# Raw weight quarters of a second attention unit in the exponentials' tiles, and of the first output half in a row tile

## The chip, the cores and the metric

The kernel runs on one core of a Trainium2 chip. It is one launch that computes a whole decoder layer. The metric is device time in microseconds (us): the median of three runs before is 1226.28 us (1226.03 to 1226.78). One further execution was profiled; all rows below come from it.

## The reference

The layer has a sequence of 1024 rows and 1024 columns, all in float32. Cut to what matters here:

```python
h = rms_norm(x, norm1_w[l])
proj = h @ w_in[l]
da_q, da_k, da_v, dn_qkv, dn_z, dn_a, dn_b = jnp.split(proj, [...], axis=-1)
da_q = rms_norm(da_q.reshape(B, S, DA_HEADS, 2, DA_QK_DIM), q_norm_w[l])
da_k = rms_norm(da_k.reshape(B, S, DA_HEADS, 2, DA_QK_DIM), k_norm_w[l])
da_o = diff_attention(da_q, da_k, da_v, lam)          # two softmax maps per head, 4 heads
...
dn_o = gated_delta_rule(dn_q, dn_k, dn_v, g, beta)    # chunked scan, 4 heads
...
mix = jnp.concatenate([da_o.reshape(B, S, DA_WIDTH), dn_o.reshape(B, S, DN_WIDTH)], axis=-1)
x = x + mix @ w_out[l]
h = rms_norm(x, norm2_w[l])
x = x + jnp.square(jax.nn.relu(h @ w_up[l])) @ w_down[l]
```

## The kernel before

Every large product is made of three TensorE products: an operand is split into a rounded part (H) and the rest (L), and HH, HL and LH are added up in PSUM. A weight is therefore loaded raw by DMA, ScalarE casts it to the rounded part (`wH`, L213) and VectorE or GpSimd subtracts to get the rest (`wL`, L214). `load_unit` (L199) does that in quarters: DMA into a raw buffer, cast, subtraction.

The stages follow each other: the first projections; the DeltaNet heads' projections; then, between 213 and 444 us, a stage in which several streams share TensorE; then the output projection, still beside attention; then the MLP from about 615 us to the end.

In the shared stage run: `horner` (a triangular inverse, in four tiles of the tag `pexp`), `scan` and `scan_out` (the DeltaNet scan in eight chunks), `da_units` (attention's projections), `da_turns` (their transposes, L947 and L948, and the split of what comes out into `qa`, L954 and L955), `scores` (L1130 to L1149) and `values` (L1171 to L1190). The order of TensorE's instructions is written out by a planner, the class `Interleave`: streams with priorities run against a modelled clock, and `unit_time` (L753) tells it when each quarter of a weight is due. The other engines' orders are set by the framework's scheduler from dependences; each engine, and SP's queue of DMA issues, then works its own list in order.

`da_units` works on three weight units of 512 columns. A unit has two halves of the contraction, `kh` 0 and 1, each of four k steps; a k step is three matmuls of 512 columns (L994, L995, L996). Eight token tiles go through in four pairs, so a unit is 64 k steps; below, "second unit, step 5" counts them from 0 in the order in which they are made: two tiles' `kh` 0 (four steps each), then their `kh` 1. Each finished tile is copied out of one of two PSUM banks by ScalarE (`qn`, L1022). A half's weights for the next unit may be cast as soon as the last pair is through with that half, and they are due when the next unit's first pair comes to them.

A raw quarter before has one of two buffers:

```python
raw = rp.tile([P, 2 * UC], F32, tag="wraw", name="wraw", bufs=5) if rp else laid("wraw")
```

`laid("wraw")` has two buffers, so the third and the fourth quarter of a half can only be fetched once the first and the second have been subtracted. The planner has the same in `start = flow.now if i < 2 else done[i - 2]`.

A turn (L947, L948) needs one of two PSUM banks of the tag `px`, which is free again when VectorE has made the last `qa` rest (L955) of the turn two before it.

After the scan, a pool of eight row tiles holds the accumulators of the eight token tiles (`accs`), into which x is loaded ahead (L935) and to which the output projection's halves are added (L1280).

Of the kernel before, what the change touches and what calls it, by code (L numbers as in the profile page):

```python
# [9 lines left out]
F32 = mybir.dt.float32  # L10
# [8 lines left out]
P = 128  # L19
SEQ = 1024  # L20
DM = 1024
KB = DM // P
NT = SEQ // P
# [5 lines left out]
UC = 260  # L29
# [103 lines left out]
def tile_hymba_layer(  # L133
# [7 lines left out]
    V, S, G, T = nc.vector, nc.scalar, nc.gpsimd, nc.tensor  # L141
# [3 lines left out]
    w_in_v = w_in[0].rearrange("(kb p) c -> p kb c", p=P)  # L145
    w_out_v = w_out[0].rearrange("(kb p) c -> p kb c", p=P)
# [17 lines left out]
    def laid(tag):  # L164
        if tag in ahead:
            return ahead.pop(tag)
        pool, shape, dt, bufs = FORMS[tag]
        return pool.tile(shape, dt, tag=tag, name=tag, bufs=bufs)
# [27 lines left out]
    hH = hpool.tile([P, KB, SEQ], F32R, name="hH")  # L196
    hL = hpool.tile([P, KB, SEQ], F32R, name="hL")

    def load_unit(src, ranges, k0=0, nk=KB, eng=None, rp=None):  # L199
        eng = eng or G  # L200
        width = sum(n for _, n in ranges)
        wh, wl = staged("wH"), staged("wL")
        wh = wh[:, :nk * width].rearrange("p (k c) -> p k c", k=nk)
        wl = wl[:, :nk * width].rearrange("p (k c) -> p k c", k=nk)
        st = 2 * UC // width
        for k in range(0, nk, st):
            raw = rp.tile([P, 2 * UC], F32, tag="wraw", name="wraw", bufs=5) if rp else laid("wraw")
            raw = raw[:, :st * width].rearrange("p (k c) -> p k c", k=st)
            o = 0
            for c0, n in ranges:  # L210
                nc.sync.dma_start(raw[:, :, o:o + n], src[:, k0 + k:k0 + k + st, c0:c0 + n])
                o += n
            S.copy(wh[:, k:k + st, :], raw)  # L213
            eng.tensor_tensor(wl[:, k:k + st, :], raw, wh[:, k:k + st, :].bitcast(F32), ALU.subtract)  # L214
        return wh, wl
# [144 lines left out]
    with tc.manual_schedule(engines={T.engine, V.engine, S.engine}):  # L360
# [37 lines left out]
        raw = n1.tile([P, NT, UC], F32, name="zr")  # L398
# [17 lines left out]
    for tb in range(NT):  # L416
        T.matmul(tail[:, 300 + 2 * tb:302 + 2 * tb], ssum_[:, tb * P:(tb + 1) * P], ones[:, 0:2],
                 start=True, stop=True)
# [310 lines left out]
    ae = actx.enter_context(tc.tile_pool(name="ae", bufs=4, **right))  # L729
# [16 lines left out]
    flow = Interleave()  # L746
# [3 lines left out]
    HF = (slice(0, 64), slice(64, 128))  # L750
    MM, TR = 219.0, 110.0

    def unit_time(eng="G", rate=1230.0):  # L753
        done = []
        for i in range(4):
            start = flow.now if i < 2 else done[i - 2]
            done.append(flow.chain(("S", 520.0), (eng, rate), start=start + DMA_T))
        return done

# [112 lines left out]
    def scan_out(c, Sold, yy):  # L872
        pkb = {}
        for h in range(HEADS):
            pkb[h] = sb.tile([P, 2, P], F32, tag="pkb", name="pkb", bufs=5)
            nc.sync.dma_start(pkb[h], park_d[h, c, :, 3:5, :])
        zgt = sb.tile([P, 512], F32, tag="zgt", name="zgt", bufs=1)
        nc.sync.dma_start(zgt, zg_d[c])
        flow.begun(("oc", c % 2))
        oc = sb.tile([P, 512], F32, tag="oc", name="oc", bufs=2)  # L880
        so = sb.tile([P, 4], F32, tag="so", name="so", bufs=2)
        osq = sb.tile([P, P], F32, tag="osq", name="osq", bufs=1)
        yield flow.now + 2500, "pB"
        if c > 0:
            o1 = pB.tile([P, 512], F32, tag="pB", name="ps_o1")
            for h in range(HEADS):
                T.matmul(o1[:, h * P:(h + 1) * P], pkb[h][:, 0, :], Sold[h], start=True, stop=True)
            V.tensor_tensor(v4(oc), v4(o1), bc_col(eg[:, c::8]), ALU.mult)
            flow.pe(4 * MM)
            flow.hold("pB", flow.chain(vec(512)))  # L890
            yield flow.now, "pB"
        o2 = pB.tile([P, 512], F32, tag="pB", name="ps_o2")
        for h in range(HEADS):
            T.matmul(o2[:, h * P:(h + 1) * P], pkb[h][:, 1, :], yy[h], start=True, stop=True)
        if c > 0:
            V.tensor_tensor(oc, oc, o2, ALU.add)
        else:
            S.copy(oc, o2)
        for h in range(HEADS):
            i = cidx(h, c)  # L900
            S.activation(osq, oc[:, h * P:(h + 1) * P], AF.Square, scale=rq[:, i:i + 1], accum_out=so[:, h:h + 1])
        f = sb.tile([P, 4], F32, tag="of", name="of", bufs=2)
        rstd(f, so, 1.0 / P, EPS, sb, "oft", 4)
        V.tensor_tensor(f, f, rqr[:, c::8], ALU.mult)
        for h in range(HEADS):
            V.scalar_tensor_tensor(oc[:, h * P:(h + 1) * P], oc[:, h * P:(h + 1) * P], f[:, h:h + 1],
                                   zgt[:, h * P:(h + 1) * P], ALU.mult, ALU.mult)
        flow.pe(4 * MM)
        t = flow.chain(vec(512))
        flow.hold("pB", t)  # L910
        t = flow.chain(*[act(P, True)] * 4, vec(4), powr(4), vec(4), *[vec(P, 60)] * 4, start=t)
        flow.put_off(t, ("oc", c % 2), lambda: nc.sync.dma_start(mixn_d[c], oc))
        if c == NT - 1:
            yield t + DMA_T, None
            flow.begun(("oc", c % 2))
            s2ctx.close()
            spctx.close()
            mp = ctx.enter_context(tc.tile_pool(name="mp", bufs=1, **left))
            pools["mp"] = mp
            for tb in tiles:  # L920
                accs[tb] = row_tile("acc")
            pools["a2"] = bctx.enter_context(tc.tile_pool(name="a2", bufs=1, **left))
            pools["be"] = bctx.enter_context(tc.tile_pool(name="be", bufs=2, **left))
            pools["rsc"] = scctx.enter_context(tc.tile_pool(name="rsc", bufs=1, space=PSUM, **right))
            state["scan"] = True

    def row_tile(name):
        return pools["mp"].tile([P, DM], F32, tag="row", name=name, bufs=8)

    def prefetch_x(after):  # L930
        if state["scan"] and state["xs"] < NT:
            tb = state["xs"]
            state["xs"] += 1
            with tc.issue_after(after.ins):
                nc.sync.dma_start(accs[tb], x2[tb * P:(tb + 1) * P, :])  # L935
# [33 lines left out]
    def da_units():  # L969
        todo = [[(512, 256), (0, 256)], [(1024, 256), (768, 256)], [(1280, 256), (256, 256)]]  # L970

        def half_w(src, ranges, k0):
            return load_unit(src, ranges, k0, 4, eng=V), unit_time("V", 610.0)

        w = [(w, [0.0] * 4) for w in first_w]
        freed = [0.0, 0.0]
        for i in range(3):
            if i == 1:
                vts[0] = ap.tile([P, NT, P], F32, tag="vt", name="vt")
            for pair in range(NT // 2):  # L980
                pss = {}
                for kh in range(2):
# [18 lines left out]
                            freed[j] = yield from leave(i, tb, ps)  # L1001
                    if pair == NT // 2 - 1:
                        if i < 2:
                            w[kh] = half_w(w_in_v, todo[i + 1], 4 * kh)
                        elif kh == 0:
                            pre.append(half_w(w_out_v, [(0, 512)], 4))
        pctx.close()
        state["proj"] = True

# [251 lines left out]
    def outproj():  # L1261
# [39 lines left out]

        w0 = pre[0]
        w1 = load_unit(w_out_v, [(512, 512)], 4, 4), unit_time()
        while state["xs"] < NT:
            tb = state["xs"]
            state["xs"] += 1
            nc.sync.dma_start(accs[tb], x2[tb * P:(tb + 1) * P, :])
        for n in range(2):
# [177 lines left out]
    pre = []  # L1486
# [350 lines left out]
```

## Time and profile before

| what | value |
|---|---|
| median of three runs | 1226.28 us |
| the profiled execution | 1228.35 us, its span 1226.6 us, granted clock 1.00 |
| TensorE (PE) busy | 1212.7 us, 99% of the span |
| VectorE (DVE) busy | 849.7 us, 69% |
| ScalarE (ACT) busy | 605.4 us, 49% |
| share of the chain that ended last | PE 91%, DVE 3%, DMA 2%, ACT 2% |
| PE busy from 300 to 310 and 310 to 320 us | 9.49 and 8.84 of 10 us |

A row of a timeline gives the start, the duration, the engine, the line, the operation with what it writes and reads, and in brackets the idle time of the engine before it with what ended it. SPq is SP issuing a DMA. A matmul's end is modelled: 512-wide matmuls start 0.23 us apart and are shown 0.39 us long, so a pause of PE shows as idle only in so far as it is longer than that overlap. Engines other than PE may idle at no cost.

### The profile page before, as it was taken

The numbers are of one execution on the slowest core, as the hardware profiler recorded it, in microseconds if no ns is written. First come the engines' busy times: TensorE is split into PE (matmuls) and PEld (weight loads), VectorE is DVE, ScalarE is ACT, GpSimd is POOL, SyncE is SP. The second block draws the span as 40 slices with busy tenths as digits, with TensorE's granted clock in tenths as the row PEclk, the third lists the DMA queues.
The fourth block names the chain that finished last, engine by engine and source line by source line (L and its number), as shares of the span: only waits on it lengthen the run. The fifth ranks groups of instructions, "written<-read, shape, count | busy, mean of one in ns | idle before, by whom it ended". The sixth has DMA issues, their size and how long they took to land.

```text
span 1226.6 us, 17630 instructions
## 1 busy us (share of the span) xinstructions
PE 1212.7 (99%) x6331; PEld 1028.6 (84%) x6331; DVE 849.7 (69%) x1445; ACT 605.4 (49%) x1173; POOL 120.7 (10%) x162
## 2 busy tenths in 40 slices
PE   9999999999999999999999999999999999999998
PEld 9988888898788888888788888888888888888887
DVE  7687788478868577766798554565577955786553
ACT  7565544234456555656566444454563333333331
POOL 0011110223332231212100000000000000000000
PEclk9999999999999999999999999999999999999999
DMA  6564442457755674334528433443279855433401
GB/s 229 163 187 129 115 128 83 123 157 242 231 164 176 183 243 137 109 84 144 183 86 282 163 123 137 172 172 137 103 250 345 330 187 184 162 103 103 137 35 69
DMA packets 160783, 199.04 MB, mean 162 GB/s; under 512 B 20960, under 2 KB 120632, under 8 KB 160696
## 3 DMA queue, kind: packets, MB, share of 16 engines
q1 hardware_dynamic: 160696, 197.92, 49.2%
q8 instruction: 50, 0.82, 0.3%
q14 instruction: 37, 0.30, 0.1%
HBM read 132.32 MB, written 65.56 MB: 161 GB/s over the span
## 4 chain that ended last, share of the span: by engine, by line
PE 91%; DVE 3%; DMA 2%; ACT 2%; issue 1%; POOL 0%; SPq 0%; ACTq 0%; POOLq 0%; DVEq 0%
PE X L1436 5%; PE X L1435 5%; PE X L1434 5%; PE X L1750 4%; PE X L1751 4%; PE X L1752 4%; PE ps_dn L221 4%; PE ps_dn L220 4%; PE ps_dn L219 4%; PE ps_qk L994 3%; PE ps_qk L996 3%; PE ps_qk L995 3%; PE Y L1436 3%; PE Y L1435 3%; PE Y L1434 3%; PE ps_o L1183 2%
## 5 line engine op out<-in xcount | busy, mean ns | idle before, releaser
L1353 ACT CAST hH<-ur 128x1024 fp32r<-128x1024 f32 x56 | 58.7, 1050 | 166.0 <-PE X L1751 79.1
L1354 DVE TENSOR_TENSOR hL<-ur,hH 128x1024 fp32r<-128x1024 f32 x56 | 68.3, 1223 | 78.6 <-ACT hH L1353 78.6
L1354 DVE TENSOR_TENSOR op<-raw,op 128x1024 fp32r<-128x1024 f32 x48 | 58.7, 1223 | 75.1 <-PE X L1435 42.1
L1750 PE MATMUL X<-hH 128*128 128x512 f32 x224 | 87.1, 389 | 0.0
L1751 PE MATMUL X<-hL,hH 128*128 128x512 f32 x224 | 87.1, 389 | 0.0
L1752 PE MATMUL X<-hH,hL 128*128 128x512 f32 x224 | 87.1, 389 | 0.0
L994 PE MATMUL ps_qk<-wH,hH 128*128 128x512 f32 x192 | 81.9, 427 | 0.7 <-ACT qn L1022 0.7
L995 PE MATMUL ps_qk<-wL,hH 128*128 128x512 f32 x192 | 75.3, 392 | 1.2 <-DVE wL L214 1.2
L219 PE MATMUL ps_dn<-hH,wH 128*128 128x512 f32 x192 | 75.9, 395 | 0.0
L220 PE MATMUL ps_dn<-hL,wH 128*128 128x512 f32 x192 | 75.6, 394 | 0.0
L996 PE MATMUL ps_qk<-wH,hL 128*128 128x512 f32 x192 | 75.5, 393 | 0.0
L221 PE MATMUL ps_dn<-hH,wL 128*128 128x512 f32 x192 | 75.4, 393 | 0.0
L1354 DVE TENSOR_TENSOR hL<-dw,hH 128x1024 fp32r<-128x1024 f32 x56 | 68.2, 1219 | 2.8 <-ACT hH L1353 2.7
L1353 ACT CAST op<-raw 128x1024 fp32r<-128x1024 f32 x48 | 50.5, 1052 | 34.7 <-PE Y L1436 19.9
L1353 ACT CAST hH<-dw 128x1024 fp32r<-128x1024 f32 x56 | 58.6, 1047 | 16.7 <-PE X L1752 5.2
L1139 ACT ACTIVATE pexp<-ps_sc,mx 128x128 f32<-128x128 f32 (+7 forms) x64 | 47.3, 741 | 26.3 <-DVE mx L1135 26.2
L577 DVE SCALAR_TENSOR_TENSOR cy<-cp,pv,cy 128x512 f32<-128x512 f32 x72 | 53.9, 748 | 8.4 <-ACT cy L575 7.5
L1135 DVE TENSOR_REDUCE mx<-ps_sc 128x1 f32<-128x128 f32 (+7 forms) x64 | 47.5, 754 | 14.2 <-PE ps_sc L1133 13.7
L1273 PE MATMUL ps_op<-wH,hH 128*128 128x512 f32 x128 | 53.6, 419 | 0.0
L1275 PE MATMUL ps_op<-wH,hL 128*128 128x512 f32 x128 | 50.3, 393 | 0.0
L1274 PE MATMUL ps_op<-wL,hH 128*128 128x512 f32 x128 | 50.0, 391 | 0.0
L1434 PE MATMUL Y<-hH,op 128*128 128x512 f32 x128 | 49.8, 389 | 0.0
(355 smaller groups left out, 3382.3 us busy)
## 6 DMA issues: line engine op xcount, KB each, us to landing
ur<-ud SPq DMA_DIRECT2D x28, 1024.0 KB, 5.0
raw<-in_w_up_dram SPq DMA_DIRECT2D x32, 512.0 KB, 3.8
dw<-in_w_down_dram SPq DMA_DIRECT2D x32, 512.0 KB, 7.2
qk_d<-qa SPq DMA_DIRECT2D x32, 256.0 KB, 2.7
ud<-ua SPq DMA_DIRECT2D x16, 512.0 KB, 4.0
ud<-s SPq DMA_DIRECT2D x16, 512.0 KB, 2.6
wraw<-in_w_in_dram SPq DMA_DIRECT2D x24, 256.0 KB, 3.3
wraw<-in_w_in_dram SPq DMA_DIRECT2D x48, 128.0 KB, 2.6
```

The source lines that it names most:

```text
L219: T.matmul(ps, lh(k), rh(k), start=(k == 0), stop=False)
L220: T.matmul(ps, lh(k), rl(k), start=False, stop=False)
L221: T.matmul(ps, ll(k), rh(k), start=False, stop=(k == n - 1))
L994: T.matmul(ps, hH[:, 4 * kh + k, sl], wh[:, k, :], start=(kh + k == 0), stop=False)
L995: T.matmul(ps, hH[:, 4 * kh + k, sl], wl[:, k, :], start=False, stop=False)
L996: T.matmul(ps, hL[:, 4 * kh + k, sl], wh[:, k, :], start=False, stop=(kh + k == 4))
L1353: S.copy(dst[0], src)
L1354: V.tensor_tensor(dst[1], src, dst[0].bitcast(F32), ALU.subtract)
L1434: T.matmul(ps, op[0][:, k, cs], h[0][:, k, :], start=start and k == 0, stop=False, skip_group_check=True)
L1750: T.matmul(o, v[0][:, j, sl], v[2][:, j, c], start=s0, stop=False, skip_group_check=True)
L1751: T.matmul(o, v[0][:, j, sl], v[3][:, j, c], start=False, stop=False, skip_group_check=True)
L1752: T.matmul(o, v[1][:, j, sl], v[2][:, j, c], start=False, stop=s1, skip_group_check=True)
```

## The change

For the second attention unit (`i == 0` when it is fetched), the third and the fourth raw quarter of each half go to a tile of 1024 columns of the exponentials' tag `pexp` (named `more`, two of the four buffers, one for each half), not to `wraw`. For the first half of the output projection's weights they go to a row tile that is taken first from the pool of eight; the eighth accumulator (`tiles[7]`, token tile 0) is then taken later, behind that tile, and its x is loaded by the loop that followed the prefetches before. The prefetches of x run in the order of `tiles` (7 down to 1). The planner is told four buffers (`ring=4`) at these two places. The third unit keeps two buffers. No computation is added or left out.

```diff
-    def load_unit(src, ranges, k0=0, nk=KB, eng=None, rp=None):
+    def load_unit(src, ranges, k0=0, nk=KB, eng=None, rp=None, more=None):
...
         for k in range(0, nk, st):
-            raw = rp.tile([P, 2 * UC], F32, tag="wraw", name="wraw", bufs=5) if rp else laid("wraw")
+            if more is not None and k > 1:
+                raw = more[:, 512 * (k - 2):512 * (k - 1)]
+            else:
+                raw = rp.tile([P, 2 * UC], F32, tag="wraw", name="wraw", bufs=5) if rp else laid("wraw")
...
-    def unit_time(eng="G", rate=1230.0):
+    def unit_time(eng="G", rate=1230.0, ring=2):
         done = []
         for i in range(4):
-            start = flow.now if i < 2 else done[i - 2]
+            start = flow.now if i < ring else done[i - 2]
             done.append(flow.chain(("S", 520.0), (eng, rate), start=start + DMA_T))
...
             pools["mp"] = mp
-            for tb in tiles:
+            pools["more"] = row_tile("more")
+            for tb in tiles[:7]:
                 accs[tb] = row_tile("acc")
...
     def prefetch_x(after):
-        if state["scan"] and state["xs"] < NT:
-            tb = state["xs"]
+        if state["scan"] and state["xs"] < NT - 1:
+            tb = tiles[state["xs"]]
...
-        def half_w(src, ranges, k0):
-            return load_unit(src, ranges, k0, 4, eng=V), unit_time("V", 610.0)
+        def half_w(src, ranges, k0, more=None):
+            return load_unit(src, ranges, k0, 4, eng=V, more=more), unit_time("V", 610.0, 2 if more is None else 4)
...
                         if i < 2:
-                            w[kh] = half_w(w_in_v, todo[i + 1], 4 * kh)
+                            more = ae.tile([P, SEQ], F32, tag="pexp", name="more") if i == 0 else None
+                            w[kh] = half_w(w_in_v, todo[i + 1], 4 * kh, more)
                         elif kh == 0:
-                            pre.append(half_w(w_out_v, [(0, 512)], 4))
+                            pre.append(half_w(w_out_v, [(0, 512)], 4, pools["more"]))
...
         w1 = load_unit(w_out_v, [(512, 512)], 4, 4), unit_time()
+        accs[tiles[7]] = row_tile("acc")
         while state["xs"] < NT:
-            tb = state["xs"]
+            tb = tiles[state["xs"]]
```

The changed kernel's lines stand 3 to 6 further down (L213 becomes L216, L214 L217, L954 L958, L955 L959, L994 L998, L1022 L1027). From the end of the first unit on, the planner writes TensorE's order anew; the order is the same again where the third unit ends, in what has been done by then.

The first place is ScalarE where the first unit ends and the second begins. `wH0` is the rounded half `kh` 0, `wH1` that of `kh` 1, `qn_3526` the last tile but one of the first unit and `qn_3612` its last. Before:

```order
L1022 ACTIVATE qn_3526<-ps_qk_3406,rt_133 128x512
L213 CAST wH0_3484<-wraw_3496 128x512
L213 CAST wH0_3484<-wraw_3501 128x512
L954 ACTIVATE qa_3563<-ps_qkt_3560,pv_575 64x256
L954 ACTIVATE qa_3590<-ps_qkt_3587,qw_578 64x256
L954 ACTIVATE qa_3563<-ps_qkt_3560,pv_575 64x256
L901 ACTIVATE osq_3472,so_3471<-oc_3470,small2_73 128x128
L1022 ACTIVATE qn_3612<-ps_qk_3429,rt_133 128x512
L213 CAST wH1_3627<-wraw_3629 128x512
L901 ACTIVATE osq_3472,so_3471<-oc_3470,small2_73 128x128
L954 ACTIVATE qa_3590<-ps_qkt_3587,qw_578 64x256
L213 CAST wH1_3627<-wraw_3634 128x512
```

And in the changed kernel, where the last tile is `qn_3581`:

```order
L216 CAST wH0_3485<-wraw_3492 128x512
L216 CAST wH0_3485<-more_3484 128x512 x2
L958 ACTIVATE qa_3476<-ps_qkt_3473,qw_578 64x256
L1027 ACTIVATE qn_3525<-ps_qk_3406,rt_133 128x512
L958 ACTIVATE qa_3562<-ps_qkt_3559,pv_575 64x256
L958 ACTIVATE qa_3573<-ps_qkt_3570,qw_578 64x256
L958 ACTIVATE qa_3562<-ps_qkt_3559,pv_575 64x256
L1027 ACTIVATE qn_3581<-ps_qk_3429,rt_133 128x512
L216 CAST wH1_3597<-wraw_3599 128x512
L216 CAST wH1_3597<-wraw_3604 128x512
L216 CAST wH1_3597<-more_3596 128x512 x2
L958 ACTIVATE qa_3573<-ps_qkt_3570,qw_578 64x256
```

The casts of a half stand together, and the last tile's copy no longer stands behind a square of the scan (`osq`).

The second place is VectorE behind that, from the first unit's last products on. `wL1` is the rest of `kh` 1, `oc` and `sy` are the scan's. Before (two more subtractions of `wL1`, each with other work ahead of it, follow further down):

```order
L1034 TENSOR_REDUCE sn_3528<-qsq_3532 128x4
L955 SCALAR_TENSOR_TENSOR qa_3563<-ps_qkt_3560,pv_575,qa_3563 64x256
L896 TENSOR_TENSOR oc_3470<-oc_3470,ps_o2_3568 128x512
L955 SCALAR_TENSOR_TENSOR qa_3590<-ps_qkt_3587,qw_578,qa_3590 64x256
L244 TENSOR_SCALAR rnt_3536<-sn_3528 128x8
L848 COPY sy_2565<-ps_A_2566 128x512
L955 SCALAR_TENSOR_TENSOR qa_3563<-ps_qkt_3560,pv_575,qa_3563 64x256
L214 TENSOR_TENSOR wL1_3628<-wraw_3629,wH1_3627 128x512
L1039 TENSOR_TENSOR qn_3526<-qn_3526,rn_3535 128x256 x2
L955 SCALAR_TENSOR_TENSOR qa_3590<-ps_qkt_3587,qw_578,qa_3590 64x256
L1034 TENSOR_REDUCE sn_3614<-qsq_3615 128x4
L214 TENSOR_TENSOR wL1_3628<-wraw_3634,wH1_3627 128x512
```

Now:

```order
L1039 TENSOR_REDUCE sn_3527<-qsq_3531 128x4
L959 SCALAR_TENSOR_TENSOR qa_3573<-ps_qkt_3570,qw_578,qa_3573 64x256
L247 TENSOR_SCALAR rnt_3535<-sn_3527 128x8
L959 SCALAR_TENSOR_TENSOR qa_3562<-ps_qkt_3559,pv_575,qa_3562 64x256
L899 TENSOR_TENSOR oc_3470<-oc_3470,ps_o2_3618 128x512
L217 TENSOR_TENSOR wL1_3598<-wraw_3599,wH1_3597 128x512
L217 TENSOR_TENSOR wL1_3598<-wraw_3604,wH1_3597 128x512
L1044 TENSOR_TENSOR qn_3525<-qn_3525,rn_3534 128x256 x2
L217 TENSOR_TENSOR wL1_3598<-more_3596,wH1_3597 128x512 x2
L1039 TENSOR_REDUCE sn_3583<-qsq_3584 128x4
L851 COPY sy_2565<-ps_A_2566 128x512
L959 SCALAR_TENSOR_TENSOR qa_3573<-ps_qkt_3570,qw_578,qa_3573 64x256
```

All four subtractions of the half come at once, and the last rest of the turn `qa_3573`, which empties a `px` bank, has moved behind them.

The third place is TensorE there, from the second unit's step 5 on. Before, the two turns stand apart:

```order
L996 MATMUL ps_qk_3663<-wH0_3484,hL_102 128x512
L857 MATMUL ps_A_2566<-sy_2565,pka_3424 128x128 x4
L947 MATMUL ps_qkt_3696<-ident_103,qn_3526 128x128
L948 MATMUL ps_qkt_3696<-ident_103,qn_3526 128x128
L994 MATMUL ps_qk_3663<-wH0_3484,hH_101 128x512
L995 MATMUL ps_qk_3663<-wL0_3485,hH_101 128x512
L996 MATMUL ps_qk_3663<-wH0_3484,hL_102 128x512
L947 MATMUL ps_qkt_3707<-ident_103,qn_3526 128x128
L948 MATMUL ps_qkt_3707<-ident_103,qn_3526 128x128
```

Now they stand together, behind step 7:

```order
L1000 MATMUL ps_qk_3662<-wH0_3485,hL_102 128x512
L951 MATMUL ps_qkt_3675<-ident_103,qn_3525 128x128
L952 MATMUL ps_qkt_3675<-ident_103,qn_3525 128x128
L951 MATMUL ps_qkt_3683<-ident_103,qn_3525 128x128
L952 MATMUL ps_qkt_3683<-ident_103,qn_3525 128x128
L998 MATMUL ps_qk_3637<-wH1_3597,hH_101 128x512
```

The second of them takes the bank that `qa_3573` above has to give back. On SP's queue the eight fetches into `more` for the second unit stand among the scan's loads of its third chunk, far ahead of the seam.

## The prediction

> **What bounds the kernel now.** The page first: which engine fills the span, and which of its groups idle.
>
> ```profile
> span 1226.6 us, 17630 instructions
> PE 1212.7 (99%) x6331; PEld 1028.6 (84%) x6331; DVE 849.7 (69%) x1445; ACT 605.4 (49%) x1173; POOL 120.7 (10%) x162
> ...
> L994 PE MATMUL ps_qk<-wH,hH 128*128 128x512 f32 x192 | 81.9, 427 | 0.7 <-ACT qn L1022 0.7
> L995 PE MATMUL ps_qk<-wL,hH 128*128 128x512 f32 x192 | 75.3, 392 | 1.2 <-DVE wL L214 1.2
> ...
> wraw<-in_w_in_dram SPq DMA_DIRECT2D x48, 128.0 KB, 2.6
> ```
>
> TensorE is the bound everywhere. The change takes no matmul away, so it can only win or lose pauses of PE, of which there are 13.9 us (1226.6 less 1212.7) in the whole program. The view of PE's waits says where the larger ones are:
>
> ```profile
> PE ps_sc L1130 <- ACT pexp L1139: 1.5, 2, 0.9
> PE ps_qk L995 <- DVE wL L214: 1.2, 2, 1.0
> PE ps_at L1171 <- DVE pexp L1149: 0.9, 1, 0.9
> PE ps_tr L1366 <- DVE hL L259: 0.9, 1, 0.9
> ```
>
> Only the second row is a wait for a weight, twice, 1.2 us in all: that is all the change can aim at by itself. The timeline shows the longer of the two, at the seam of the first and second unit.
>
> ```profile
> 297.87 1.13 ACT L213 CAST wH<-wraw 128x512 fp32r<-128x512 f32 x2
> 299.86 1.29 DVE L214 TENSOR_TENSOR wL<-wraw,wH 128x512 fp32r<-128x512 f32 x2
> ...
> 300.57 1.81 SPq L211 DMA_DIRECT2D wraw<-in_w_in_dram  x4
> 300.93 0.69 ACT L1022 ACTIVATE qn<-ps_qk,rt 128x512 f32<-128x512 f32 x1 [0.61 <-PE ps_qk L996]
> ...
> 305.33 1.26 ACT L213 CAST wH<-wraw 128x512 fp32r<-128x512 f32 x2 [3.70 <-DMA wraw<-in_w_in_dram]
> ...
> 308.65 0.39 PE L994 MATMUL ps_qk<-wH,hH 128*128 128x512 f32 x1
> 309.10 0.39 PE L996 MATMUL ps_qk<-wH,hL 128*128 128x512 f32 x1
> 309.43 0.69 ACT L1022 ACTIVATE qn<-ps_qk,rt 128x512 f32<-128x512 f32 x1
> 310.17 0.50 PE L994 MATMUL ps_qk<-wH,hH 128*128 128x512 f32 x1 [0.68 <-ACT qn L1022]
> ...
> 316.72 0.62 ACT L213 CAST wH<-wraw 128x512 fp32r<-128x512 f32 x1 [1.03 <-DMA wraw<-in_w_in_dram]
> 318.25 0.40 PE L994 MATMUL ps_qk<-wH,hH 128*128 128x512 f32 x1
> 318.90 0.68 DVE L214 TENSOR_TENSOR wL<-wraw,wH 128x512 fp32r<-128x512 f32 x1
> 319.64 0.50 PE L995 MATMUL ps_qk<-wL,hH 128*128 128x512 f32 x1 [0.99 <-DVE wL L214]
> 321.34 0.69 DVE L888 TENSOR_TENSOR oc<-ps_o,eg 128x512 f32<-128x512 f32 x1
> 321.38 0.40 PE L996 MATMUL ps_qk<-wH,hL 128*128 128x512 f32 x1
> 322.08 1.16 PE L894 MATMUL ps_o<-sy,pkb 128*128 128x128 f32 x8 [0.31 <-DVE oc L888]
> ```
>
> The ring of two is seen at work. Casts and subtractions of two quarters, then the fetch (300.57), and ScalarE stands 3.70 us until the next two have landed. In `kh` 1 it happens again, 1.03 us ahead of the last cast, and the fourth quarter is subtracted at 318.90 to 319.58, when PE already waits. Matmuls of 512 columns start 0.225 us apart (308.65 to 309.10 are two), so the delays are: 309.10 to 310.17 less 0.23 = 0.84 us (the last tile's copy, late on ScalarE); 318.25 to 319.64 less 0.23 = 1.16 (the fourth quarter); 321.38 to 322.08 less 0.23 = 0.47 (VectorE late with the scan).
>
> **The change part by part: the seam.** The four fetches into `more` of each half need only tiles of the inverse that is long done; they are issued among the scan's loads and cost SP's queue eight issues, for which nothing on PE waits. The other rows that I need for the new order:
>
> ```profile
> 302.97 0.27 PE L947 MATMUL ps_qkt<-ident,qn 128*128 128x128 f32 x1
> 303.06 0.86 DVE L838 SCALAR_TENSOR_TENSOR sr<-ps_A,neg_eg,pka 128x128 f32<-128x128 f32 x3
> 303.18 1.06 PE L894 MATMUL ps_o<-sy,pkb 128*128 128x128 f32 x8
> 304.08 0.27 PE L947 MATMUL ps_qkt<-ident,qn 128*128 128x128 f32 x1
> 307.23 0.41 DVE L1034 TENSOR_REDUCE sn<-qsq 128x4 f32<-128x256 f32 x1
> 307.68 0.48 DVE L955 SCALAR_TENSOR_TENSOR qa<-ps_qkt,pv,qa 64x256 fp32r<-64x256 f32 x1
> 308.19 0.47 ACT L954 ACTIVATE qa<-ps_qkt,pv 64x256 fp32r<-64x256 f32 x1 [0.87 <-DVE qa L955]
> 309.41 0.17 DVE L244 TENSOR_SCALAR rnt<-sn 128x8 f32<-128x8 f32 x1
> 311.34 1.17 DVE L1039 TENSOR_TENSOR qn<-qn,rn 128x256 f32<-128x256 f32 x2
> ```
>
> A k step is 3 x 0.23 = 0.69 us, a turn 0.21 (302.97 to 303.18), a group of four scan products 0.90 (303.18 to 304.08). TensorE's order is the old one up to the turn at 302.97, so I walk on from there by the new lists. PE: turn to 303.2, step, turn, last step of the first unit to 304.8, scan group to 305.7, steps 0 and 1 to 307.1, scan group to 308.0, steps 2 and 3 to 309.4, steps 4 to 7 to 312.1, then two turns.
>
> VectorE: four subtractions from 299.86, 0.645 each, to 302.4 (two of them moved up); rest of `qa` 302.9; `oc` 303.6 (0.69, as at 321.34); four `sr` (0.29 each) and one `sn` 305.15; rest of `qa_3562` 305.6. ScalarE: four casts from 297.87, 0.565 each, to 300.1; `qn` of the last tile but one at 300.93, when PE is through with it; the second part of `qa_3562` waits for VectorE until 305.6, to 306.1; then the last tile's `qn`, to 306.8. Step 4 wants that bank at 309.4: **the 0.84 us go**, with 2.6 us to spare. Then four casts to 309.1, and the second part of `qa_3573` to 309.5.
>
> VectorE again from 305.6: `sn` 306.0, `qa` 306.5, `rnt` 306.7, `qa` 307.2, `oc` 307.9, two subtractions 309.2, two normings 310.4, two subtractions 311.6. The fourth quarter is needed at step 11, after 314: **the 1.16 us go**. But behind these stand `sn` 312.0, `sy` (0.69, as `oc`) 312.7 and only then the last rest of `qa_3573`, 313.2, which gives the `px` bank back. The second of the two turns wants it at 312.3: **a new wait of 0.9 us**, behind which all of PE queues. Its bounds: nothing if ScalarE and VectorE run 0.9 us ahead of my lists, 1.6 if one 0.69 us operation more gets in front.
>
> The 0.47 us at 322.08 go too: between that chunk's first and second output group PE now has a turn, six k steps and a group (5.2 us), against two groups' worth and four steps before, and no subtraction of a weight is left in front of the scan's `oc`. Bounds: 0 to -0.47.
>
> **The third unit** keeps its ring of two. Its wait:
>
> ```profile
> 389.30 0.40 PE L994 MATMUL ps_qk<-wH,hH 128*128 128x512 f32 x1
> 389.86 0.50 PE L995 MATMUL ps_qk<-wL,hH 128*128 128x512 f32 x1 [0.16 <-DVE wL L214]
> ```
>
> That is 0.56 less 0.23 = 0.33 us, for the third quarter of `kh` 1. In the new order five value products (0.22 each by the scan's groups of four) stand ahead of it and two transposes (0.1 each) fewer, 0.9 us more cover: -0.33, bounds 0 and -0.33.
>
> **The output half** gains nothing by itself:
>
> ```profile
> 443.09 0.62 ACT L213 CAST wH<-wraw 128x512 fp32r<-128x512 f32 x1 [0.48 <-DMA wraw<-in_w_out_dram]
> 444.68 0.68 DVE L214 TENSOR_TENSOR wL<-wraw,wH 128x512 fp32r<-128x512 f32 x1
> 447.27 0.44 PE L1130 MATMUL ps_sc<-KS,qa 128*128 128x384 f32 x1 [0.58 <-ACT pexp L1139]
> 450.20 0.48 PE L1273 MATMUL ps_op<-wH,hH 128*128 128x512 f32 x1
> ```
>
> Its last quarter is ready at 445.36 and first needed after 450.20. What goes is a subtraction (0.68) in front of the scores' maxima; what comes on ScalarE is two casts of the second half (1.13) ahead of the exponential whose bank PE waits for at 447.27. They end about when that exponential started. I take 0, bounds -0.5 and +1.1. The eighth accumulator's load waits for the fourth subtraction; it is used seven tiles later, and costs nothing. The x prefetches only change their order.
>
> **The rest** of the reordered stretch (322 to 615 us) keeps its work, but its pauses are dealt anew. Of the waits above, 1.5 + 0.9 + 0.9 us stand there, with the smaller ones about 6 us as delays. I see no reason for more or for fewer and take 0, bounds -6 and +6.
>
> **Sum:** -0.84 - 1.16 - 0.47 - 0.33 + 0.9 = -1.9 us. The profiled span goes from 1226.6 to 1224.7. The profiled execution took 1228.35 us, 1.75 over its span; the median of the runs is 1226.28, so on it the forecast is 1224.4 us.
>
> One figure of a page can be held against the fetch. The Trainium skill, DMA: Bandwidth & Descriptors, "Anatomy of one DMA", fits a transfer (on GpSimd's path; here SP issues) as 2.0 us plus bytes over 436 GB/s, by my estimate 2.3 us for 128 KB, where the page of the profile has 2.6. By it the two ring turns would be 0.6 us shorter, the wait removed 0.56 in place of 1.16, and the sum -1.3. No row here shows so short a median, so the row decides.
>
> **The rivals.** (a) *The dealing helps too.* For it: the second unit's weights no longer tie the scan's and the scores' VectorE work down, and the three largest other waits are on just that work. Against: ScalarE and VectorE do the same operations. With half of the 6 us gone: 1226.28 - 1.9 - 3.0 = 1221.4.
>
> (b) *Given back.* The seam's gain only brings PE earlier to the next wait on ScalarE or VectorE, which end when they did. For it: their lists are unchanged in length, and the stage's waits all name them. Against: they idle (69% and 49% busy). Time: 1226.3.
>
> (c) *The bursts block the queues*, slower. Casts and subtractions come four at a time, 2.26 us on ScalarE and 2.58 on VectorE, at three places (two halves of the second unit, the output half), and whatever PE waits for stands behind them, as `qa_3573` does. I price one such place at 0.9. If two more cost a whole burst, it is 0.9 + 2 x 2.58 = 6.1 against 2.8 gained: 1226.28 + 3.3 = 1229.6. It decides from 5.3 us of new waits on. For it: 308.19, where ScalarE stood 0.87 us behind a wait with a copy for PE behind it. Against: in the walk above the bursts had slack at two of three uses.
>
> The Trainium skill has the rule for (c): TensorE: Matmul & The Clock Gate, "Architectural detail", says that ScalarE's and VectorE's queues are strictly first in, first out. By that rule the burst is paid in full wherever its followers have no slack. The trace agrees at 308.19 to 309.43.
>
> (d) *The planner hides the change*, since it was told of four buffers and now counts on weights that the queues deliver later: that would leave a wait L995 <- L214 at the seam. By the walk 3 us are to spare, so I leave it at the edge of (b).
>
> **How the numbers follow.** Forecast 0.50, with its own range 1222.8 to 1226.0; (a) 0.22; (b) with (d) 0.14; (c) 0.14. About 0.2%, 2.45 us, is what a measurement can tell from no change: faster is below 1223.8, slower above 1228.7. Of the forecast case 0.15 lies below 1223.8; with (a) that makes 0.37 faster. (c) gives 0.13 slower. The rest, 0.50, is the same. The range for 8 in 10 takes in most of (a) and (b) and the foot of (c): 1220.6 to 1228.4.
>
> **What would show it.** In the waits after: no L1027 wait at the seam, no L217 wait for the second unit (a later one for the third unit would leave that step wrong), and a new one of the turn L951 on a `qa` rest of about 0.7 us idle. Casts into `wH1` back to back without a DMA as releaser. The two waits of L1130 near 447 still there. Wrong it is if PE's waits from 322 to 615 us differ by more than 2 us in sum from before, or if the seam's turn waits longer than 1.6.

## The result: slower by 0.39%, and the profile after

The changed kernel takes 1231.93 us (median of 6 runs, 1228.53 to 1233.09) against 1226.43 us before (6 runs): a ratio of 1.0039, 95% interval 1.0029 to 1.0050. By the ratio that is slower by 4.8 us (5.5 by the medians), where 1.9 us less was forecast. Each ratio below is to runs of the kernel before that were made along with it; their medians went from 1226.11 to 1227.39 us, so the ratios are to be compared, not medians of different runs. The profiled execution took 1232.57 us with a span of 1230.8, 4.2 us more than the one of before.

The page of the changed kernel, and the view of PE's waits:

```profile
span 1230.8 us, 17601 instructions
PE 1211.3 (98%) x6331; PEld 1029.4 (84%) x6331; DVE 848.8 (69%) x1445; ACT 604.5 (49%) x1173; POOL 122.1 (10%) x162
...
PE ps_at L1176 <- ACT om L1194: 3.5, 2, 1.9
PE ps_qkt L951 <- DVE qa L959: 2.5, 1, 2.5
PE ps_sc L1135 <- ACT pexp L1144: 1.7, 3, 0.9
...
PE ps_tr L1372 <- ACT hn L1373: 1.6, 1, 1.6
...
PE ps_at L1176 <- DVE hL L265: 1.1, 1, 1.1
```

The waits for weights (L995 on L214 before) are gone altogether, and so is the one for the last tile's copy (L1022, now L1027). Larger ones have come: a turn for a `qa` rest, two transposes of the exponentials for `om`, one of the MLP's transposes for `hn`. The waits of the scores for an exponential, which the prediction left in place, are still there (L1135).

The seam in the timeline of the changed kernel, rows left out:

```profile
303.43 0.33 SPq L963 DMA_DIRECT2D qk_d<-qa  x1
...
304.58 0.47 ACT L958 ACTIVATE qa<-ps_qkt,pv 64x256 fp32r<-64x256 f32 x1 [2.44 <-DMA qk_d<-qa]
...
308.08 0.47 ACT L958 ACTIVATE qa<-ps_qkt,qw 64x256 fp32r<-64x256 f32 x1 [3.03 <-DMA qk_d<-qa]
...
309.65 1.13 ACT L216 CAST wH<-wraw 128x512 fp32r<-128x512 f32 x2
310.42 1.71 DVE L217 TENSOR_TENSOR wL<-wraw,wH 128x512 fp32r<-128x512 f32 x2
310.68 1.14 ACT L216 CAST wH<-more 128x512 fp32r<-128x512 f32 x2
312.05 0.75 DVE L1044 TENSOR_TENSOR qn<-qn,rn 128x256 f32<-128x256 f32 x2
312.72 1.28 DVE L217 TENSOR_TENSOR wL<-more,wH 128x512 fp32r<-128x512 f32 x2
313.92 0.41 DVE L1039 TENSOR_REDUCE sn<-qsq 128x4 f32<-128x256 f32 x1
314.25 0.68 DVE L851 COPY sy<-ps_A 128x512 f32<-128x512 f32 x1
314.96 0.49 DVE L959 SCALAR_TENSOR_TENSOR qa<-ps_qkt,qw,qa 64x256 fp32r<-64x256 f32 x1
315.59 0.45 PE L951 MATMUL ps_qkt<-ident,qn 128*128 128x128 f32 x1 [2.54 <-DVE qa L959]
316.48 0.63 PE L999 MATMUL ps_qk<-wL,hH 128*128 128x512 f32 x1
316.90 0.63 PE L1000 MATMUL ps_qk<-wH,hL 128*128 128x512 f32 x1
```

The buffers do what they were to do: the four casts stand together, none waits for a DMA. The second turn waits for the last `qa` rest behind the burst, as the walk had it, but for 2.54 us. Two things are new. ScalarE stood 2.44 and 3.03 us, not for a weight, but for the stores of `qa` of two turns before: `qa` has two buffers, and the store issued at 303.43 let ScalarE go on at 308.08. And behind the pause matmuls of 512 columns start 0.42 us apart (316.48 to 316.90) in place of 0.23. The view by windows has the granted clock (1.00 is full speed) as the column PEclk, behind POOL:

```profile
300.00:313.00 13.00, 13.00 (x75) 10.83 (x74) 10.61 (x23) 6.98 (x16) 3.92 (x4) 1.00 0.70 210
313.00:316.00 3.00, 0.46 (x4) 0.44 (x3) 2.90 (x7) 1.82 (x7) 0.89 (x2) 0.88 0.43 127
316.00:318.00 2.00, 2.00 (x7) 1.61 (x6) 1.37 (x6) 0.42 (x1) 2.00 (x2) 0.50 0.35 131
318.00:320.00 2.00, 2.00 (x8) 1.58 (x8) 1.91 (x6) 0.91 (x3) 0.34 (x1) 0.83 0.36 66
```

By these shares TensorE ran at half its clock for 3.4 us (0.12 x 3 + 0.50 x 2 + 0.17 x 2 us lost, over 0.5). Six starts in a row came late, one by 0.35 us and five by 0.2: 1.35 us on top of the pause.

The delays of PE, worked out as in the prediction (start to start, less the usual distance; pauses over 0.15 us), in the two profiled executions:

| place, us | before | after | difference |
|---|---|---|---|
| seam, 300 to 322 | 2.5 | 2.7 and 1.35 of slow matmuls | +1.6 |
| 338 to 345 | 1.4 | 0.9 | -0.5 |
| 380 (L1176 for `om`) | 0 | 2.0 | +2.0 |
| 389 to 392 | 0.8 | 0 | -0.8 |
| 447 to 454 | 1.8 | 2.2 | +0.4 |
| 462 | 0.5 | 1.3 | +0.7 |
| 494 to 518 | 0.8 | 1.8 | +1.0 |
| 559 to 627 | 2.5 | 2.5 | 0 |

The rows add up to 4.4 us. Up to 300 us, where TensorE's order is the same, the profiled execution after is 0.5 us later: the waits of L338 at its start were 2.0 us in all, against 0.6 before, and the clock was halved there too (PEclk 0.51 from 8 to 11.5 us, 1.00 before). The seam, and the stretch that was dealt anew, each lost where a gain or nothing was forecast.

### The profile page after: what moved, and what is told of

Its sections match the earlier page's. It is cut to its first block, busy times and chain, and to the rows that moved or that the text cites. A ratio compares the mean times of both kernels' runs of the same rounds, so it can differ in the third digit from the quotient of the medians.

```text
span 1230.8 us, 17601 instructions
## 1 busy us (share of the span) xinstructions
PE 1211.3 (98%) x6331; PEld 1029.4 (84%) x6331; DVE 848.8 (69%) x1445; ACT 604.5 (49%) x1173; POOL 122.1 (10%) x162
## 4 chain that ended last, share of the span: by engine, by line
PE 86%; DVE 5%; DMA 3%; ACT 3%; issue 2%; SPq 1%; POOL 0%; POOLq 0%; ACTq 0%; DVEq 0%
PE X L1440 5%; PE X L1442 5%; PE X L1441 5%; PE X L1757 4%; PE X L1758 4%; PE X L1756 4%; PE ps_dn L222 3%; PE ps_dn L224 3%; PE ps_dn L223 3%; PE ps_qk L998 3%; PE ps_qk L1000 3%; PE ps_qk L999 3%; PE Y L1440 2%; PE Y L1442 2%; PE Y L1441 2%; PE Z L1757 2%
## 5 line engine op out<-in xcount | busy, mean ns | idle before, releaser
L998 PE MATMUL ps_qk<-wH,hH 128*128 128x512 f32 x192 | 81.9, 427 | 0.0
```

The source lines that it names most:

```text
L998: T.matmul(ps, hH[:, 4 * kh + k, sl], wh[:, k, :], start=(kh + k == 0), stop=False)
```

## Which part, and order or buffers

Four kernels take the change apart. Two make one of its parts alone. The other two part the buffers from the planner's order: TensorE's instructions stand in the one exactly as before and in the other exactly as in the changed kernel.

**The second unit alone** (the row tile and the order of the x fetches undone):

```diff
-                            pre.append(half_w(w_out_v, [(0, 512)], 4, pools["more"]))
+                            pre.append(half_w(w_out_v, [(0, 512)], 4))
```

> Only the second attention unit's quarters are moved (and the planner told of four buffers for them); the output half stays in its ring of two. If the loss adds up from both parts, as the pauses of the two profiles say (seam +1.7 us by 2.70 and 1.5 against 2.47; 338 to 344 us -0.5; 380 us +2.0; 390 us -0.8), this part alone is 2.4 us slower than before: 1228.8 us, with the wait of L951 at the seam and the wait of L1176 near 380 us. If the output half is what loses, it is at 1226.4 or below.

Measured: 1227.89 us (11 runs), ratio to before 1.0005 (0.9997 to 1.0014). No change that can be told, where 2.4 us were expected: the pause at the seam was 1.19 us in its profile, without slow matmuls behind it, and the one near 380 us 1.1 us. That profile is of the fastest of the eleven runs, one of two at a granted clock of 1.00; the nine others were at 0.997 to 0.999, and what their pauses were is not known.

**The output half alone**:

```diff
-                            more = ae.tile([P, SEQ], F32, tag="pexp", name="more") if i == 0 else None
-                            w[kh] = half_w(w_in_v, todo[i + 1], 4 * kh, more)
+                            w[kh] = half_w(w_in_v, todo[i + 1], 4 * kh)
```

> Only the output half's quarters are moved; the second unit stays in its ring of two, and TensorE's order is the old one up to the third unit's end. If both parts lose, this one is 2.2 us slower than before (447 to 454 us +0.4, 462 us +0.7, 495 to 518 us +1.0, and nothing in sum from there on): 1228.6 us. If the seam and its clock loss are all of it, 1226.4.

Measured: 1230.78 us (8 runs), 1.0035 (1.0022 to 1.0049). This part, which I had costed at nothing, loses by itself nearly as much as the whole change.

**All buffers, the planner told of two**, so that TensorE's order is the old one from first to last:

```diff
-            return load_unit(src, ranges, k0, 4, eng=V, more=more), unit_time("V", 610.0, 2 if more is None else 4)
+            return load_unit(src, ranges, k0, 4, eng=V, more=more), unit_time("V", 610.0, 2)
```

> All buffers are moved as in the change, but the planner is still told of two, so that TensorE's order is the old one from first to last. If the written order is what loses, the buffers alone take away the waits for the weights (1.16 and 0.33 us) and add none: 1224.9 us, at most 1226.4. If the bursts of casts and subtractions lose by themselves, whatever TensorE's order, it is near the change: 1229 to 1232 us.

Measured: 1226.73 us (11 runs), 0.9998 (0.9989 to 1.0006). The same as before.

**The old buffers, the planner told of four** (on the kernel before, at the second unit and the output half), so that TensorE's order is the changed kernel's:

```diff
-                            w[kh] = half_w(w_in_v, todo[i + 1], 4 * kh)
+                            w[kh] = half_w(w_in_v, todo[i + 1], 4 * kh, 4 if i == 0 else 2)
...
-                            pre.append(half_w(w_out_v, [(0, 512)], 4))
+                            pre.append(half_w(w_out_v, [(0, 512)], 4, 4))
```

> The buffers are those of before, but the planner is told of four, so that TensorE's order is the changed kernel's from first to last. If the written order is what loses, this is as slow as the change or slower by the weights' waits that stay (1.2 us): 1231 to 1234 us. If the bursts lose, it is at 1226 to 1228 us.

Measured: 1233.90 us (6 runs), 1.0062 (1.0043 to 1.0080).

So the loss is the order's. It costs 0.62% with the old buffers, 0.41% with the new ones (1.0039 over 0.9998). That the buffers give back 0.2% of it in the new order is hardly told from nothing (the intervals of 1.0062 and 1.0039 overlap); in the old one they give nothing. Bursts of casts and subtractions lose nothing by themselves: they are all there in the run with the old order.

In the kernel with the output half alone, the profiled execution shows what such an order does (its timeline, engines mixed):

```profile
624.13 0.40 PE L1441 MATMUL Y<-hH,wL 128*128 128x512 f32 x1
624.86 0.62 ACT L1358 CAST wH<-wraw 128x512 fp32r<-128x512 f32 x1 [3.36 <-DMA wraw<-in_w_up_dram]
625.39 0.61 ACT L1358 CAST T0h<-hn 128x512 fp32r<-128x512 f32 x1
625.91 0.58 ACT L1372 COPY hn<-ps_tr 128x512 f32<-128x512 f32 x1
...
626.54 0.68 PE L1371 MATMUL ps_tr<-ident,hn 128*128 128x128 f32 x4 [2.01 <-ACT hn L1372]
626.95 0.70 PE L1439 MATMUL Y<-hH,wL 128*128 128x512 f32 x1
627.45 0.63 PE L1440 MATMUL Y<-hL,wL 128*128 128x512 f32 x1
```

ScalarE waits for an MLP weight with the copy behind it that frees a bank, and PE has nothing left ahead of the transpose. In the kernel before, the same wait of ScalarE fell behind the last of these transposes, so that nobody waited (its timeline):

```profile
619.25 0.60 PE L1366 MATMUL ps_tr<-ident,hn 128*128 128x128 f32 x4
...
621.28 0.62 ACT L1353 CAST wH<-wraw 128x512 fp32r<-128x512 f32 x1 [1.50 <-DMA wraw<-in_w_up_dram]
```

At 461 us (`hL`, on VectorE) and 516 us (`om`, on ScalarE) PE also stands for a bank whose release is late, though not for a weight.

## The wait behind the wait at the seam

That the buffers bring nothing even in the old order had to have a cause of its own. Around the seam, in that run (planner told of two), ScalarE's waits and PE's pause read, in the timeline:

```profile
302.46 0.47 ACT L958 ACTIVATE qa<-ps_qkt,pv 64x256 fp32r<-64x256 f32 x1 [2.56 <-PE ps_o L897]
305.86 0.47 ACT L958 ACTIVATE qa<-ps_qkt,qw 64x256 fp32r<-64x256 f32 x1 [2.93 <-DMA qk_d<-qa]
...
308.91 0.69 ACT L1027 ACTIVATE qn<-ps_qk,rt 128x512 f32<-128x512 f32 x1
...
309.65 0.50 PE L998 MATMUL ps_qk<-wH,hH 128*128 128x512 f32 x1 [1.32 <-ACT qn L1027]
...
453.74 0.63 PE L255 MATMUL ps_tr<-ident,mt 128*128 128x128 f32 x4 [1.56 <-issue]
```

Where ScalarE waited 3.70 us for a weight before, it now waits for `qa`'s stores, and the last tile's copy is late by that. (The row at 302.46 names PE as what came last; in the kernel with the tile below, where this copy needs no store, it starts at 301.61.) To take this wait away, the `qa` of turns 10 and 11 (the two at the seam) goes into a further tile of the exponentials' tag; two more buffers, and no other edit:

```diff
-            qa = sd.tile([P, 2, 256], F32R, tag="qa", name="qa", bufs=2)
+            if state["turned"] == 10:
+                pools["qx"] = ae.tile([P, SEQ], F32R, tag="pexp", name="qx")
+            if state["turned"] in (10, 11):
+                n0 = 512 * (state["turned"] - 10)
+                qa = pools["qx"][:, n0:n0 + 512].rearrange("p (m c) -> p m c", m=2)
+            else:
+                qa = sd.tile([P, 2, 256], F32R, tag="qa", name="qa", bufs=2)
```

**On the changed kernel:**

> The changed kernel, and turns 10 and 11 (the two at the end of the first unit) write their qa into a tile of the exponentials instead of the ring of two, so that ScalarE need not wait there until the stores of turns 8 and 9 have landed (2.44 and 3.03 us in the profile of the change). TensorE's order is the changed kernel's. If those waits make the seam's pause so long, the pause of L951 falls from 2.5 us to 0.9 us or less, TensorE's clock stays up behind it, and the time falls by 1.8 to 3.3 us against the change: about 1229 us. If the burst of four subtractions makes it, the pause stays near 2.5 us and the time at 1231 to 1232 us.

Measured: 1228.42 us (12 runs), 1.0016 (1.0001 to 1.0030), by the ratios 0.23% or 2.8 us less than the change. In its profile, of the second fastest of the twelve runs, PE does not wait at all for a `qa` rest, and the clock stays at 1.00 (by windows):

```profile
300.00:330.00 30.00, 29.55 (x176) 25.44 (x175) 25.77 (x66) 14.80 (x40) 10.41 (x11) 1.00 0.72 230
```

Six of its twelve runs had a granted clock of 1.00, none of the six of the changed kernel. The tile moves one more thing: four of the eight fetches into `more`, issued near 250 us in the changed kernel, are issued at 301.73 us here, and a cast waits 0.50 us for one of them (at 307.16), PE for none.

How much the store matters shows in two profiles without the tile and with the same order of TensorE up to here: the changed kernel and the second unit alone. Their views of DMA issues give the time from issue to landing as the last figure, for the store at 303.43 us in the one and 302.55 us in the other; the rows of ScalarE are of the second unit alone:

```profile
qk_d<-qa SPq DMA_DIRECT2D x1, 256.0 KB, 4.5
...
qk_d<-qa SPq DMA_DIRECT2D x1, 256.0 KB, 3.1
...
303.57 0.47 ACT L957 ACTIVATE qa<-ps_qkt,pv 64x256 fp32r<-64x256 f32 x1 [2.30 <-DMA qk_d<-qa]
305.77 0.47 ACT L957 ACTIVATE qa<-ps_qkt,qw 64x256 fp32r<-64x256 f32 x1 [1.74 <-DMA qk_d<-qa]
```

The store landed 1.4 us sooner after its issue, and the turn's delay was 1.35 us in place of 2.70. So the stores made the seam's long pause; the burst was only what stood between.

**On the buffers with the old order:**

> All buffers of the change with the order of before (planner told of two), and the same tile for turns 10 and 11. There ScalarE waited 2.56 and 2.93 us, and TensorE 1.48 us for the last tile's copy L1027 behind it and 0.47 us for the scan's product. If the stores are what took back the seam's gain, both pauses go and the time is 1.5 to 2 us under that run: about 1225 us, faster than before by 0.15%. If the copy L1027 is late for another reason, it stays at 1226.7 us.

Measured: 1225.38 us (11 runs), 0.9979 (0.9970 to 0.9988). Faster than before. In its timeline:

```profile
303.30 0.47 ACT L964 ACTIVATE qx<-ps_qkt,qw 64x256 fp32r<-64x256 f32 x1 [1.23 <-PE ps_qkt L952]
...
306.90 0.69 ACT L1033 ACTIVATE qn<-ps_qk,rt 128x512 f32<-128x512 f32 x1
307.49 1.13 ACT L216 CAST wH<-wraw 128x512 fp32r<-128x512 f32 x2
...
307.90 0.39 PE L1006 MATMUL ps_qk<-wH,hL 128*128 128x512 f32 x1
308.12 0.39 PE L1004 MATMUL ps_qk<-wH,hH 128*128 128x512 f32 x1
```

ScalarE waits for PE now, not for a store; the copy is there 2 us earlier, and the matmul behind it starts on time. The 0.47 us of the scan's product at 301.9 stayed, against what was expected of this run (0.48 us, PE for `oc`).

**The tile alone, on the kernel before:**

> The kernel before, with nothing but the tile of the exponentials for the qa of turns 10 and 11. If ScalarE's waits at the seam stand in series (first for the weight's fetch, 3.70 us, and only behind that for qa's store), the tile alone brings nothing, since the fetch still holds ScalarE: 1226.4 us, the same as before. If the stores alone were the limit, it is as fast as the buffers with the tile: 1225.0 us.

Measured: 1226.29 us (11 runs), 1.0001 (0.9992 to 1.0010). Nothing, as expected, and the waits of ScalarE there (299 to 312 us) say why:

```profile
ACT wH L213 <- DMA wraw<-in_w_in_dram: 4.7, 1, 4.7
ACT qx L960 <- DVE qx L961: 0.9, 1, 0.9
```

The fetch of the weight holds ScalarE alone. The two waits stand in series: each edit by itself measures zero (0.9998 and 1.0001), and both together gain 0.21%.

**Without the output half's row tile:**

> The second unit's quarters in the exponentials' tiles, the qa tile for turns 10 and 11, the order of before (planner told of two); the output half stays in its ring of two, without the row tile. If the gain is made at the seam alone, this is as fast as with the output half's buffers: 1225.4 us. If the output half's buffers have a part in it, it lies between that and before: 1226 us.

Measured: 1223.42 us (11 runs), 0.9979 (0.9970 to 0.9988). The output half's buffers have no part in the gain. In the profiles they even cost: PE's delays between 442 and 458 us are 0.58, 1.02 and 1.56 us with them and 0.59, 1.02 and 0.54 without, 1.0 us more. The third is the pause shown above at 453.74, for which the profile names no releaser ("issue"). These transposes need a bank of the tag `px`, and they start 0.10 us after VectorE has ended a `qa` rest, at 453.64 us in the run without the `qa` tile and at 451.27 us in the one with it: most likely it is a wait for that bank. The ratios of the two kernels, 0.9979 both, do not show it. This version, or the one with the row tile, beats both kernels of the case.

## Other orders of the output stage

If the order costs, is it this order, or would any other do the same? The planner's order of the output stage does not hang on when the half's weights are due: with these times moved by 0.5 to 2 us either way, the written order stays that of before, instruction for instruction. With the modelled fetch moved, and with it the slots that the casts and subtractions take on ScalarE and VectorE in the planner's model, it is dealt anew. Two such draws, both with all buffers of the change and two told elsewhere:

```diff
-            return load_unit(src, ranges, k0, 4, eng=V, more=more), unit_time("V", 610.0, 2 if more is None else 4)
+            return load_unit(src, ranges, k0, 4, eng=V, more=more), unit_time("V", 610.0, 2, 2000.0 if src is w_out_v else DMA_T)
```

where the last argument of `unit_time` takes the place of `DMA_T` in it (2500 ns). In the second draw it is 4000.

> All buffers of the change, the planner told of two, but for the output half it counts with 2.0 us for a fetch in place of 2.5. No wait is removed or added by it, and TensorE's order changes from the third unit's end on, about as much as with four buffers (774 against 789 instructions). If any new order of the output stage costs, as a draw against one that was well chosen, this is 1 to 7 us slower than the same buffers in the old order: 1228 to 1234 us. If the order that comes of four buffers is bad in itself, this is as likely below as above 1226.7 us, within 2 us.

Measured: 1227.94 us (10 runs, 1226.51 to 1233.66), 1.0009 (0.9997 to 1.0021): not told from before. The profiled execution is the slowest of the ten; it has pauses of 1.9 us at 461 us and 2.6 us at 626 us with slow matmuls behind both. The four runs at a granted clock of 1.00 took 1226.5 to 1227.4 us, the six at 0.996 to 0.998 took 1227.4 to 1233.7: what this order loses, if anything, goes with the clock.

> All buffers of the change, the planner told of two, but for the output half it counts with 4.0 us for a fetch in place of 2.5. This deals the output stage a third order (608 instructions off that of before, and 450 to 500 off those of the other two draws). If the order of before is simply better dealt than most, it is again slower than the same buffers in the old order (1226.7 us): 1228 to 1231 us. If what costs is one pattern that the other two draws share (long pauses near 461 and 626 us), this one is without it and within 1 us of 1226.7.

Measured: 1233.29 us (5 runs), 1.0055 (1.0042 to 1.0068). It has neither of these two pauses, but others (its view of PE's waits):

```profile
PE ps_tr L1372 <- DVE hL L262: 5.8, 1, 5.8
PE ps_tr L255 <- issue: 2.8, 1, 2.8
```

With the output half alone that makes three orders of this stage, at 1.0009, 1.0035 and 1.0055, against 0.9998 for the old order with all buffers. The first two are relatives: by the traces some 90 of TensorE's 6331 instructions stand elsewhere, against 250 to 470 between any other two of the four. None is better, one cannot be told from the old one, and two lose 0.35 and 0.55%. That the old one is the best of many is not shown by three, and neither is what a new order costs on the mean. Why each has its pauses, and whether anything in the order foretells them, stays open.

## What a pause does to TensorE's clock

> Nothing of the layer is computed: x is passed through, and TensorE runs 48 blocks of 32 to 38 matmuls of 512 columns with pauses between them that VectorE sets by 1 to 16 small operations, about 1 to 4 us, each length three times. If a pause of some 2 us can halve the clock, as behind the 2.54 us at the seam and the 2.01 us near 626 us (but not behind 1.85 us), matmuls 0.43 us apart follow some of the pauses from 2 us on, for about 3.4 us. The Trainium skill (TensorE: Matmul & The Clock Gate, "What's actually happening") says at least one idle window of about 3.4 us: by that none follows a pause under 3.4 us.

The span of this kernel is 603.7 us; it ran once, as did the next one. Two of its blocks of 32 matmuls, behind a short and a longer pause (timeline of PE; merged rows):

```profile
20.95 7.56 PE L157 MATMUL ps<-s,identr 128*128 128x512 f32 x32 [0.78 <-DVE s L158]
30.60 9.18 PE L157 MATMUL ps<-s,identr 128*128 128x512 f32 x32 [2.09 <-DVE s L160]
```

The second block takes 1.6 us longer. Counted over all 48 pauses, by their idle time: after 0.8 to 1.8 us (15 pauses) no block was slowed; after 2.1, 2.4, 2.6 and 2.9 us (3 each) 8 of 12; after 3.1 us and more all 21. A slowed block loses mostly 1.6 to 1.8 us against one that was not, at most 2.9.

> Nothing of the layer is computed: x is passed through, and TensorE runs 45 blocks of 36 to 42 matmuls with two equal pauses behind each, 0.9 to 2.0 us long, 2, 4 or 8 matmuls apart (0.4 to 1.8 us). Single pauses of 0.94 to 1.99 us never halved the clock. If it goes by the idle time within one stretch of some 3.4 us, pairs of 1.2 to 2.0 us that stand close (2 or 4 matmuls apart) halve it at times, and those 8 apart less often. If it goes by a single pause, no pair here halves it, apart perhaps from those of 1.99 us.

Pairs of pauses of 0.8 to 1.6 us each slowed 11 of 24 blocks where 2 or 4 matmuls lay between, and none of 12 where there were 8 (1.8 us). With 1.8 us each it was 8 of 9, whatever lay between. So pauses add up over a short stretch: two of 0.8 us, 1.6 us of idle time together, did it in 2 of 6 cases, where a single one of 1.8 us never did. A sharp bound does not come out of these counts; from 3.1 us on a single pause did it every time.

In the layer 2.54 us and 2.01 us (the rows above) halved the clock. Near 1.9 us it went either way: 1.87 us at 461 us did in the run with 2000 ns, 1.97 us at 312 us in the same profile did not, nor did 1.85 us at 380 us in the changed kernel. Short pauses add up there too: with the old buffers and the new order no pause at the seam is longer than 1.57 us, but 0.17, 0.25, 0.35 and 1.41 us stand between 315.5 and 319.4 us, and the clock (the last figure but two, by windows) was halved for two stretches:

```profile
313.40:318.70 5.30, 3.81 (x14) 2.01 (x14) 4.22 (x14) 2.59 (x6) 2.61 (x2) 1.00 0.61 171
318.70:322.20 3.50, 2.81 (x8) 2.33 (x9) 2.20 (x5) 1.26 (x3) 0.57 (x1) 0.51 0.73 228
322.20:325.60 3.40, 3.40 (x13) 2.91 (x13) 1.53 (x6) 0.00 (x0) 0.40 (x2) 0.50 0.73 244
```

The Trainium skill, TensorE: Matmul & The Clock Gate, "What's actually happening", says that the clock is halved after at least one idle window of about 3.4 us and that the windows run freely. That the same pause has either outcome agrees with free windows; the length does not agree: two thirds of the pauses from 2.1 to 2.9 us did it here, and so did two of six pairs of 0.8 us.

## Why the prediction was wrong, by its own steps

Two steps failed, the new wait of the turn and the rest dealt anew. In the two profiles each missed by about 3 us: the seam, forecast at -1.6, came out at +1.6, and the rest with the third unit, forecast at -0.3, at +2.9. Both signs of being wrong that the prediction names came: the turn waited 2.54 us, more than 1.6, and PE's waits from 322 to 615 us rose from 5.2 to 7.4 us of idle time.

- **Weights and copies at the seam** (-0.84, -1.16, -0.47): right. None of the three waits is left in the profile after.
- **The new wait of the turn** (+0.9, bounds 0 and 1.6): the right place, but a chain with a link left out, and so mis-sized. It was 2.70 us as a delay, 4.05 with the slow matmuls. The walk let ScalarE make the copies of turns 10 and 11 as soon as PE had transposed and VectorE was through, and left out that each needs the store of two turns before to have landed (waits of 2.44 and 3.03 us). The trace of before had the store at the seam: issued at 302.48, landed 4.1 us later, but hidden behind the wait for the weight. The planner counts 2.5 us for it (`DMA_T`, at `qa_free`). In the kernel with the second unit alone, with TensorE's order the same up to there, the waits were 2.30 and 1.74 us and the pause 1.19 us: the 0.9 was not far from the good case, and the landing of a store decides between the two. That a pause over 2 us can also slow what follows was not in the sum.
- **The third unit** (-0.33): right; no such wait after.
- **The output half** (0, bounds -0.5 and +1.1): at the upper bound in the profiles (+1.0 between 442 and 458 us with the order held), not seen in the times. That the size is near the bound is luck: the two waits for the exponential, on which the bound was worked out, stayed as they were (0.59 and 1.02 us against 0.58 and 1.02), and the pause at 453.74 came instead.
- **The rest, dealt anew** (0, bounds -6 and +6): this is the other step that failed. "I see no reason for more or for fewer": the delays there were 7.8 us before (not about 6) and 10.7 after in the profiles, and the order alone costs 0.4 to 0.6% in the runs, the seam's share included. I walked the new order at the seam and nowhere else, though it was at hand up to 627 us, and the place where a bank's release stands behind a wait for a weight (626 us) is on it.
- **The rivals.** (a) had the right term with the wrong sign. (b) is what the buffers do in the old order, by a mechanism that it did not name (the stores). (c) came nearest in time, 1229.6 against 1231.9 us, but for a wrong reason: with the bursts and the old order nothing is lost. (d) did not happen: no wait for a weight came back. A rival "dealt worse" was missing: the bound of +6 on the rest had room for it, but the range ended at 1228.4 and left it out.

## What to carry to other kernels

Where an edit also changes what a planner or scheduler is told, time the two apart: the same buffers with the old order, and the new order with the old buffers. A wait that is taken away shows the next one in its queue: before it is costed as a gain, look what the waiting engine's following instructions need (here a store that must have landed), and try both edits together, since each alone may measure nothing. A pause near 2 us or more, or several short ones close together, can cost more than its length, since TensorE's clock may be halved behind it.

## What the runs showed of the hardware that was not expected

Beside the clock: how long a store takes to give its buffer back varies, between profiles and within one. The same store at the seam let ScalarE go 4.65 us after its issue in the changed kernel (303.43 to 308.08) and 3.2 us in the one with the second unit alone (302.55 to 305.77); a later one in the changed kernel let it go after 2.1 us (315.48 to 317.58).

Much of the spread of the runs goes with the granted clock, which is on record for each. The changed kernel took 1228.5 us at 0.999 and 1231.6 to 1233.1 us at 0.997; the output half alone 1229.1 to 1231.0 us at 1.00 and 1232.1 to 1235.2 us at 0.996 to 0.998. The second unit's buffers with the `qa` tile, which had 1.00 in ten runs of eleven, ran from 1222.6 to 1224.8 us. The clock is not all of what the new order costs: with the old buffers it took 1232.9 and 1234.9 us in the two runs at 1.00.
